# Order of VectorE's low parts and output additions in an encoder block's attention steps, and the queue of one input load

## The chip, the cores and the metric

The kernel runs on one core of one Trainium2 chip. The metric is the device time of one launch in microseconds (us); before the change three runs gave a median of 1334.39 us (1333.94 to 1335.63). PE is the matrix engine, PEld its weight load, DVE the vector engine, ACT the scalar (activation) engine, POOL GpSimd, SP the engine that issues most DMAs.

## The reference

An encoder block on 1024 tokens of width 1024, in float32: a layer norm, one wide input projection, two attention branches side by side (2-D neighbourhood attention with a bias table, 8 heads; sliding-window attention with a sink logit, 8 query heads on 2 key heads), gates, an output projection, and a squared-ReLU MLP, with two more layer norms.

```python
h = layer_norm(x, ln0_g, ln0_b)
proj = h @ w_in[l] + b_in[l]
qa, ka, va, qb, kb, vb, ga, gb = jnp.split(proj, IN_SPLITS, axis=-1)
...
y_na = neighbourhood_attention(qa, ka, va, na_rpb[l]) @ w_branch_na[l]
y_swa = windowed_gqa_with_sink(qb, kb, vb, swa_sink[l]) @ w_branch_swa[l]
mixed = jax.nn.sigmoid(ga) * y_na + jax.nn.sigmoid(gb) * y_swa
attn_out = mixed @ w_out[l] + b_out[l]
h = layer_norm(DEEPNORM_ALPHA * h + attn_out, ln1_g[l], ln1_b[l])
u = jnp.square(jax.nn.relu(h @ w_ff1[l] + b_ff1[l]))
h = layer_norm(DEEPNORM_ALPHA * h + u @ w_ff2[l] + b_ff2[l], ln2_g[l], ln2_b[l])
```

## The kernel before

Float32 accuracy is had from a faster matmul format by splitting every operand into a high part (rounded) and a low part (the rest), and adding two or three products. The high part is mostly made by ACT, the low part by DVE as "value minus high part".

**Start.** The input is loaded in eight tiles of 128 rows (`ln`, L172 to L177), the first of them in two halves, all by SP's queue; ACT's queue loads the identity (`ident`, L181). DVE takes the statistics of each tile (L129 to L131), POOL and ACT normalise it, PE transposes it, and ACT and DVE write it as high and low parts `hT` (L251 to L255). From there the projections run: `gemm3_steps` (L283) yields one matmul at a time, 24 to a half.

**Attention steps.** There are 16 heads (0 to 7 sliding window, 8 to 15 neighbourhood), of four steps each, each step two blocks of 128 queries. Between the matmuls of the steps the projections of later heads are filled in, 12 matmuls a step for the first eight heads and 18 for the others (`pump`). The order on every engine is the order of the code (the schedule is manual), and each engine works its queue off in that order. In step s, `steps` does, in this order:

- `part_a2(s + 1)`: DVE adds the sink's term, takes the reciprocal (L592, L593) and scales the exponentials (L596);
- `part_a(s + 2)`: PE makes the scores in two `ps_s` banks (L559, L560), DVE adds the bias and takes the maxima (L562, read out as a second instruction), and scales them (L568, L566 for neighbourhood heads);
- a quarter of the fill; then the deferred work that is marked early;
- `part_b(s)`: PE transposes the scaled exponentials into two `ps_t` banks (L618), ACT copies them as high parts `pth` (L621), ACT takes the exponentials of step s + 2 (L580, L583), DVE makes the low parts `ptl` (L624); then the deferred work that isn't PE's;
- 45% of the fill; `part_c(s - 1)`: PE multiplies with the values into a `ps_o` bank (L654); two steps make a pair that shares one bank, and there are two banks. At the end of a pair ACT copies one half of the bank to `oT` (L660) and DVE adds the other half (L663);
- all deferred work that is due; the rest of the fill.

**Deferred work.** `defer(n, f, ...)` puts f in a list; every fill matmul counts n down by one, and the next flush after it has reached 0 runs f. A flush "early" (ahead of part_b) takes only entries marked early. The neighbourhood projections use it for what follows a finished half: `evac` (three ACT copies out of the `ps_mm` bank) at once, and four matmuls later `evac2`, the low parts of q and k (L358, L360, L362), both early. Other deferred work on DVE: the low weights (`wlo`, L515), the rotary shuffles and low parts (L418, L471) and the values' low parts (`vv`, L332). The output addition L663 is deferred by 0, which is the flush right behind part_c.

**After the steps** DVE forms sums of operands for the gates' projections (a scheme with seven products in place of eight; L926 and around), then come the branch and output projections and the MLP (L1351, L1784), where PE has one matmul behind the other.

Of the kernel before, what the change touches and what calls it, by code (L numbers as in the profile page):

```python
# [47 lines left out]
D_NA = 4  # L48
# [35 lines left out]
def encoder_block(ctx, tc, x, w_in, w_br, w_out, w_ff1, w_ff2, par, rows, rpbp,  # L84
                  ident_d, masks_d, rope_d, out):
    nc = tc.nc
    PE, ACT, DVE, POOL = nc.tensor, nc.scalar, nc.vector, nc.gpsimd

    def b32(ap):
        return ap.bitcast(F32)  # L90
# [12 lines left out]
    def psum(tag):  # L103
        return pp.tile([P, 512], F32, tag=tag, name=f"ps_{tag}", bufs=PSB[tag])
# [16 lines left out]
    xv = x.rearrange("(g t) d -> g t d", g=NCG)  # L121
# [34 lines left out]
    ln = r3p.tile([P, 8, D], F32, tag="r3", name="ln")  # L156
# [14 lines left out]
    def ln0_load(half):  # L171
        for g in range(half * 4, half * 4 + 4):  # L172
            if g == 0:
                for n in range(2):
                    nc.sync.dma_start(ln[:, g, n * 512:(n + 1) * 512], xv[g][:, n * 512:(n + 1) * 512])
            else:
                nc.sync.dma_start(ln[:, g, :], xv[g])  # L177

    ln0_load(0)
    ident = cp.tile([P, P], F32, name="ident")  # L180
    nc.scalar.dma_start(ident, ident_d)  # L181
# [76 lines left out]
    def h_perm(part, k, half):  # L258
        return hT[:, part, k, half * 512:(half + 1) * 512]
# [17 lines left out]
    def gemm3_steps(ps, w, act):  # L277

        hi, lo = w[:2]
        for k in range(NK):  # L280
            for i, (a, b) in enumerate(((hi, 0), (hi, 1), (lo, 0))):
                yield
                PE.matmul(ps, a[:, k, :], act(b, k), start=(k == 0 and i == 0), stop=(k == NK - 1 and i == 2))  # L283
# [6 lines left out]
    def defer(*fns, pe=False, early=False):  # L290

        later.append([fns[0], fns[1:], pe, early])
# [48 lines left out]
    def proj_na_qk(h, w, store):  # L341
        q = ap.tile([P, S], F32R, tag="q", name="q", bufs=3)
        kh = ap.tile([P, S], F32R, tag="kh", name="kh")
        kl = ap.tile([P, S], F32R, tag="kl", name="kl")
        store.append((q, kh, kl))
        bq, bk = prm[0:64, C_QK + h:C_QK + h + 1], prm[64:P, C_QK + h:C_QK + h + 1]
        for half in range(2):
            cs = slice(half * 512, (half + 1) * 512)
            ps = psum("mm")
            yield from gemm3_steps(ps, w, lambda part, k: h_perm(part, k, half))  # L350

            def evac(cs=cs, ps=ps):
                ACT.activation(q[0:64, cs], ps[0:64, :], AF.Identity, bias=bq, scale=1.0)
                ACT.activation(kh[64:P, cs], ps[64:P, :], AF.Identity, bias=bk, scale=1.0)
                ACT.activation(kh[0:64, cs], ps[64:P, :], AF.Identity, bias=bk, scale=1.0)

            def evac2(cs=cs, ps=ps):
                DVE.scalar_tensor_tensor(out=q[64:P, cs], in0=ps[0:64, :], scalar=bq, in1=b32(q[0:64, cs]),  # L358
                                         op0=ALU.add, op1=ALU.subtract)
                DVE.scalar_tensor_tensor(out=kl[64:P, cs], in0=ps[64:P, :], scalar=bk, in1=b32(kh[64:P, cs]),  # L360
                                         op0=ALU.add, op1=ALU.subtract)
                DVE.tensor_copy(kl[0:64, cs], b32(kl[64:P, cs]))  # L362
            defer(0, evac, D_NA, evac2, early=True)


    mk = ap.tile([P, 640], F32, tag="mk", name="mk", bufs=1)
# [20 lines left out]

    n_rope = [0]
    in_steps, rope_ops = [], []

    def rope_step(p):

        if rope_ops:
            j = cp.tile([P, 1], F32, tag="junk", name="junk", bufs=2)
            POOL.tensor_copy(j, p[:, 0:1])
            rope_ops.pop(0)()
            if len(rope_ops) % 5 == 1:
                rope_ops.pop(0)()
                if rope_ops:
                    defer(8, rope_ops.pop(0))  # L400
# [147 lines left out]
    def part_a(s):  # L548

        hd, t = heads[s // 4], s % 4  # L550
        (q, kh, kl), _, _, bias_of, sink_h, _, _ = hd.get()
        st = ap.tile([P, 8], F32, tag="st", name="st", bufs=4)
        pns = []
        for i in range(2):
            j = 2 * t + i
            c0, c1 = max(j - 1, 0), min(j + 2, 8)
            n = (c1 - c0) * P
            ps = psum("s")
            PE.matmul(ps[:, :n], q[:, j * P:(j + 1) * P], kh[:, c0 * P:c1 * P], start=True, stop=False)  # L559
            PE.matmul(ps[:, :n], q[:, j * P:(j + 1) * P], kl[:, c0 * P:c1 * P], start=False, stop=True)  # L560
            p = ap.tile([P, 384], F32, tag="ss", name="ss", bufs=6)
            DVE.tensor_tensor_reduce(out=p[:, :n], in0=ps[:, :n], in1=bias_of(j), scale=1.0, scalar=NEG,  # L562
                                     op0=ALU.add, op1=ALU.max, accum_out=st[:, i:i + 1])
            pns.append((p, n, c0))
        if sink_h is None:
            DVE.tensor_scalar(out=st[:, 2:4], in0=st[:, 0:2], scalar1=-0.125, scalar2=None, op0=ALU.mult)  # L566
        else:
            DVE.tensor_scalar(out=st[:, 2:4], in0=st[:, 0:2], scalar1=snk8[:, sink_h:sink_h + 1],  # L568
                              scalar2=-0.125, op0=ALU.max, op1=ALU.mult)
        hd.pairs[t] = pns, st  # L570
# [14 lines left out]
    def part_a2(s):  # L585
        if s >= 64:
            return
        hd, t = heads[s // 4], s % 4
        pns, st = hd.pairs[t]
        sink_h = hd.get()[4]  # L590
        if sink_h is not None:
            DVE.tensor_tensor(out=st[:, 4:6], in0=st[:, 4:6], in1=st[:, 6:8], op=ALU.add)  # L592
        DVE.reciprocal(out=st[:, 6:8], in_=st[:, 4:6])  # L593
        for i in range(2):
            p, n, c0 = pns[i]
            DVE.tensor_scalar(out=p[:, :n], in0=p[:, :n], scalar1=st[:, 6 + i:7 + i], scalar2=None, op0=ALU.mult)  # L596
        rope_step(p)
# [29 lines left out]
    def part_c(s):  # L627

        hd, t = heads[s // 4], s % 4
        order, pth, ptl = hd.pairs[t]  # L630
        _, vv, vi, _, _, o_chunk, o_row = hd.get()
        if t % 2 == 0:
            hd.po = psum("o")
        po = hd.po

        runs = []
        for u, (c, i) in enumerate(order):
            if runs and runs[-1][0] == c:
                runs[-1][2] += 1
            else:  # L640
                runs.append([c, u, 1, i])
        runs.sort(key=lambda r: -r[2])
        runs.append(runs.pop(1))
        cols_ = (t % 2) * 256
        nmm = 0
        for c, u, w, i in runs:
            cc = slice(cols_ + i * P, cols_ + (i + w) * P)
            vs = vv[:, c, vi, :, :].rearrange("p a f -> p (a f)")
            main = (po[:, cc], vs, pth[:, u:u + w, :].rearrange("p u f -> p (u f)"))
            corr = (po[0:64, cc], vs[:, 0:64], ptl[:, u:u + w, :].rearrange("p u f -> p (u f)"))  # L650
            nmm += 1
            lastrun = nmm == len(runs)
            for m in ((corr, main) if lastrun else (main, corr)):
                PE.matmul(*m, start=(nmm == 1 and m is main), stop=(lastrun and m is main))  # L654
        if t % 2 == 1:

            oo = oT[o_row:o_row + 64, o_chunk, (t // 2) * 512:(t // 2 + 1) * 512]

            def evac():
                ACT.copy(oo, po[64:P, :])  # L660

            def evac2():
                DVE.tensor_tensor(out=oo, in0=po[0:64, :], in1=oo, op=ALU.add)  # L663
            if s == 63:
                last_evac.extend((evac, evac2))
            else:
                evac()
                defer(0, evac2)

    def fills():  # L670
        def na_v_of(hp):
# [28 lines left out]
    with tc.manual_schedule(engines=MANUAL):  # L700
# [83 lines left out]
        def steps(s, n, before_b=None, before_c=None):  # L784

            part = [int(n * SPLIT[0]), int(n * SPLIT[1])]
            part.append(n - sum(part))
            if 0 <= s + 1 < 64:
                part_a2(s + 1)
            if s + 2 < 64:  # L790
                part_a(s + 2)
            pump(part[0])
            if before_b:
                before_b()
            flush(False, True)
            if 0 <= s < 64:
                part_b(s, lambda: part_e(s + 2))
            elif s < 0:
                part_e(s + 2)
            flush(False)  # L800
            pump(part[1])
            if before_c:
                before_c()
            if s >= 1:
                part_c(s - 1)
            flush()
            pump(part[2])
# [371 lines left out]
        for f in range(8):  # L1179
            for half in range(2):  # L1180
# [8 lines left out]
                g, h = (f, 1) if half == 0 else (f + 1, 0)  # L1189
# [871 lines left out]
```

## Time and profile before

| | |
|---|---|
| median of three runs | 1334.39 us |
| the profiled execution, by itself | 1334.06 us |
| its span in the profile | 1332.3 us |
| granted PE clock | 0.998 |
| input, norm, first projections | 0 to 86 us |
| attention steps, 12 fill matmuls each | about 86 to 249 us |
| attention steps, 18 fill matmuls each | about 249 to 450 us |
| rest | 450 to 1332 us |

The page's first part gives each engine's busy time, its share of the span and its instructions. A row of the timeline has the start in us, the duration in us, the engine, the line, the operation, what is written from what, and, where the engine was idle before, how long and for whom in brackets. A row of the waits has the waiting engine and line, whom it waited for, the sum in us, the number and the longest. A row of the groups has the count, the busy time and the mean of one in ns, and the idle time before.

### The profile page before, as it was taken

The page shows a single profiled execution, that of the slowest core. Times are in us where ns is not written, and L with a number is a line of the kernel's source. Part 1 is how long each engine was busy: PE and PEld are TensorE (multiplying, and loading weights), DVE is VectorE, ACT ScalarE, POOL GpSimd, SP SyncE. Part 2 cuts the span into 40 slices and gives each one's busy share as a digit, 9 for nine tenths or more (in the row PEclk, how much of TensorE's full clock was granted, in tenths as well). Part 3 has the DMA queues.
Part 4 walks back from the last instruction along what each step waited for, and adds up shares of the span by engine and source line. Part 5 has one row for each costly group of instructions (what it writes and reads, how often), then busy time and mean ns, then how long its engine had stood idle before and what let it go on. Part 6 is the DMA issues. An engine that isn't in the chain of part 4 may idle for free.

```text
span 1332.3 us, 17348 instructions
## 1 busy us (share of the span) xinstructions
PE 1309.4 (98%) x6296; PEld 1088.7 (82%) x6296; DVE 985.0 (74%) x1618; ACT 710.1 (53%) x1231; POOL 282.4 (21%) x279
## 2 busy tenths in 40 slices
PE   8999998999999999999999999999999999999997
PEld 6788787888888878888888888888888888888886
DVE  7758888877877896444678987677655768787778
ACT  6446666766665535542445755555555543333346
POOL 4441221121120000344540012222100001111207
PEclk9999999999999999999999999999999999999999
DMA  6521111102101323656143576655528644544323
GB/s 226 187 87 49 48 52 41 38 23 47 51 23 40 127 94 118 223 190 221 70 152 134 169 242 205 210 196 187 205 100 311 221 190 150 213 150 174 127 103 127
DMA packets 66422, 183.94 MB, mean 138 GB/s; under 512 B 10400, under 2 KB 12064, under 8 KB 60576
## 3 DMA queue, kind: packets, MB, share of 16 engines
q1 hardware_dynamic: 65904, 182.38, 39.7%
q8 instruction: 49, 0.80, 0.3%
q10 hardware_dynamic: 432, 0.46, 0.1%
q14 instruction: 37, 0.30, 0.1%
HBM read 126.69 MB, written 56.31 MB: 137 GB/s over the span
## 4 chain that ended last, share of the span: by engine, by line
PE 80%; DVE 12%; ACT 3%; issue 1%; POOL 1%; DMA 1%; SPq 0%; DVEq 0%; ACTq 0%; POOLq 0%
PE ps_mm L283 13%; PE ps_mm L1351 7%; PE ps_t L1351 6%; PE ps_o L1351 6%; PE ps_mm L1784 6%; PE ps_s L1784 6%; PE ps_o L1784 5%; PE ps_t L1784 5%; PE ps_s L1351 3%; PE ps_t L618 2%; DVE ss L562 2%; PE ps_o L654 2%; ACT ss L580 2%; PE ps_mm L886 1%; DVE ss L596 1%
## 5 line engine op out<-in xcount | busy, mean ns | idle before, releaser
L283 PE MATMUL ps_mm<-hT,whi 128*128 128x512 f32 x832 | 269.5, 398 | 2.6 <-POOL hT L255 2.1
L283 PEld LDWEIGHTS ps_mm<-hT,whi 128*128 128x128 f32 x832 | 153.6, 188 | 30.2 <-POOL hT L255 3.5
L283 PE MATMUL ps_mm<-hT,wlo 128*128 128x512 f32 x416 | 166.9, 401 | 1.0 <-DVE wlo L717 1.0
L580 ACT ACTIVATE ss<-ss,st 128x384 f32<-128x384 f32 (+1 forms) x128 | 74.5, 583 | 62.1 <-DVE st L568 47.3
L1650 ACT CAST t<-stg 128x2048 fp32r<-128x2048 f32 x28 | 53.5, 1912 | 81.9 <-PE ps_o L1784 46.3
L1803 POOL TENSOR_TENSOR acc<-acc,rst 128x512 f32<-128x512 f32 x16 | 31.0, 1934 | 293.2 <-DMA rst<-xr_d 280.7
L1784 PE MATMUL ps_mm<-t,t 128*128 128x512 f32 x384 | 89.6, 389 | 0.0
L1784 PE MATMUL ps_s<-t,t 128*128 128x512 f32 x384 | 89.6, 389 | 0.0
L283 PEld LDWEIGHTS ps_mm<-hT,wlo 128*128 128x128 f32 x416 | 78.3, 188 | 12.4 <-DVE wlo L717 1.5
L1784 PEld LDWEIGHTS ps_mm<-t,t 128*128 128x128 f32 x384 | 72.1, 188 | 14.9
L1784 PEld LDWEIGHTS ps_s<-t,t 128*128 128x128 f32 x384 | 72.1, 188 | 14.9
L1351 PE MATMUL ps_t<-hS,tw 128*128 128x512 f32 x348 | 83.6, 389 | 0.0
L1351 PEld LDWEIGHTS ps_t<-hS,tw 128*128 128x128 f32 x348 | 65.3, 188 | 13.5
L621 ACT CAST pth<-ps_t 128x384 fp32r<-128x384 f32 (+1 forms) x128 | 51.8, 454 | 43.9 <-PE ps_t L618 43.2
L1653 DVE TENSOR_TENSOR t<-stg,t 128x2048 fp32r<-128x2048 f32 x28 | 65.6, 2341 | 12.9 <-ACT t L1650 12.9
L624 DVE TENSOR_TENSOR ptl<-ps_t,pth 128x384 fp32r<-128x384 f32 (+1 forms) x128 | 61.2, 517 | 17.1 <-ACT pth L621 16.5
L1173 POOL TENSOR_TENSOR mx<-sg 128x512 f32<-128x512 f32 x16 | 33.4, 2089 | 187.8 <-DVE sg L1172 187.8
L1784 PE MATMUL ps_t<-t,t 128*128 128x512 f32 x288 | 67.8, 390 | 0.6 <-DVE t L1653 0.6
L1784 PE MATMUL ps_o<-t,t 128*128 128x512 f32 x288 | 67.2, 389 | 0.0
L1784 PEld LDWEIGHTS ps_t<-t,t 128*128 128x128 f32 x288 | 53.9, 188 | 12.6 <-DVE t L1653 1.5
L1784 PEld LDWEIGHTS ps_o<-t,t 128*128 128x128 f32 x288 | 54.1, 188 | 11.2
L1627 POOL TENSOR_TENSOR rst<-rst,rr 128x512 f32<-128x512 f32 x16 | 22.4, 1400 | 187.3 <-DMA rst<-xn_d 116.0
(307 smaller groups left out, 3159.1 us busy)
## 6 DMA issues: line engine op xcount, KB each, us to landing
us_d<-usl SPq DMA_DIRECT2D x112, 256.0 KB
stg<-us_d SPq DMA_DIRECT2D x28, 1024.0 KB
raw<-in_w_ff SPq DMA_DIRECT2D x36, 512.0 KB
raw<-in_w_in SPq DMA_DIRECT2D x28, 512.0 KB
sg<-sg_d SPq DMA_DIRECT2D x32, 256.0 KB
w2b<-in_w_ff SPq DMA_DIRECT2D x7, 1024.0 KB
w2a<-in_w_ff SPq DMA_DIRECT2D x5, 1024.0 KB
sg_d<-sa SPq DMA_DIRECT2D x16, 256.0 KB
```

The lines of the kernel that those rows point to most:

```text
L283: PE.matmul(ps, a[:, k, :], act(b, k), start=(k == 0 and i == 0), stop=(k == NK - 1 and i == 2))
L562: DVE.tensor_tensor_reduce(out=p[:, :n], in0=ps[:, :n], in1=bias_of(j), scale=1.0, scalar=NEG, op0=ALU.add, op1=ALU.max, accum_out=st[:, i ...
L580: ACT.activation(p[:, :n], p[:, :n], AF.Exp, bias=st[:, 2 + i:3 + i], scale=0.125, accum_out=st[:, 4 + i:5 + i])
L618: PE.transpose(pt[:, (u - a) * P:(u - a + 1) * P], p[:, (c - c0) * P:(c - c0 + 1) * P], ident)
L621: ACT.copy(pth[:, a:b, :], pv)
L624: DVE.tensor_tensor(out=ptl[:, a:b, :], in0=pv, in1=b32(pth[:, a:b, :]), op=ALU.subtract)
L1173: POOL.tensor_tensor(out=mx[:, f, half * 512:(half + 1) * 512], in0=both[0], in1=both[1], op=ALU.add)
L1351: PE.matmul(ps, ww, act[:, part, k, :], start=(first and k == 0 and m == 0), stop=(k == 3 and m == 2), skip_group_check=True)
L1650: ACT.copy(slot[:, :, 0, :], src)
L1653: DVE.tensor_tensor(out=slot[:, :, 1, :], in0=src, in1=b32(slot[:, :, 0, :]), op=ALU.subtract)
L1784: PE.matmul(ps, st[:, a, part, j * P:(j + 1) * P], w[:, a, wpart, :], start=(first and a == 0 and m == 0), stop=(a == 3 and m == 2), skip_ ...
L1803: POOL.tensor_tensor(out=z, in0=z, in1=t, op=ALU.add)
```

## The change

Three edits. The first tile's second half is issued by ACT's queue, ahead of the identity. The neighbourhood low parts `evac2` are marked early only when the projection's half ends in step 32 or later. The output addition is deferred by 14 fill matmuls in place of 0.

```diff
     def ln0_load(half):
         for g in range(half * 4, half * 4 + 4):
             if g == 0:
-                for n in range(2):
-                    nc.sync.dma_start(ln[:, g, n * 512:(n + 1) * 512], xv[g][:, n * 512:(n + 1) * 512])
+                for n, q in enumerate((nc.sync, nc.scalar)):
+                    q.dma_start(ln[:, g, n * 512:(n + 1) * 512], xv[g][:, n * 512:(n + 1) * 512])
...
-            defer(0, evac, D_NA, evac2, early=True)
+            defer(0, lambda: (evac(), defer(D_NA, evac2, early=step_now[0] >= 32)), early=True)
...
     in_steps, rope_ops = [], []
+    step_now = [0]
...
                 evac()
-                defer(0, evac2)
+                defer(14, evac2)
...
             part.append(n - sum(part))
+            step_now[0] = s
             if 0 <= s + 1 < 64:
```

The order of instructions on PE and POOL stays the same; ACT has one DMA issue more and SP one less; on DVE no instruction comes or goes. The first place is DVE's queue at the end of a sliding-window step, the fifth pair's output addition before, with buffer numbers. Lines behind the change are one or two higher.

```order
L624 TENSOR_TENSOR ptl_1526<-ps_t_1527,pth_1525 128x384
L624 TENSOR_TENSOR ptl_1526<-ps_t_1531,pth_1525 128x384
L663 TENSOR_TENSOR oT_844<-ps_o_1492,oT_844 64x512
L592 TENSOR_TENSOR st_1510<-st_1510 128x2
L593 RECIPROCAL st_1510<-st_1510 128x2
```

The same place on DVE in the changed kernel:

```order
L625 TENSOR_TENSOR ptl_1525<-ps_t_1526,pth_1524 128x384
L625 TENSOR_TENSOR ptl_1525<-ps_t_1530,pth_1524 128x384
L664 TENSOR_TENSOR oT_844<-ps_o_1368,oT_844 64x512
L593 TENSOR_TENSOR st_1509<-st_1509 128x2
L594 RECIPROCAL st_1509<-st_1509 128x2
```

The slot is filled as before, but with the addition of the pair before (ps_o 1368, which is 1369 in the old numbering); the fifth pair's own comes two steps later, ahead of that step's low weights. With 18 fill matmuls it comes one step later, behind the next maxima and low parts.

The second place is DVE's queue where the first half of the first neighbourhood head's projection has ended, before:

```order
L568 TENSOR_SCALAR st<-st,snk_106 128x2
L358 SCALAR_TENSOR_TENSOR q<-ps_mm,prm,q 64x512
L360 SCALAR_TENSOR_TENSOR kl<-ps_mm,prm,kh 64x512
L362 CAST kl<-kl 64x512
L624 TENSOR_TENSOR ptl<-ps_t,pth 128x384 x2
L592 TENSOR_TENSOR st<-st 128x2
L593 RECIPROCAL st<-st 128x2
```

And in the changed kernel:

```order
L569 TENSOR_SCALAR st<-st,snk_106 128x2
L625 TENSOR_TENSOR ptl<-ps_t,pth 128x384 x2
L358 SCALAR_TENSOR_TENSOR q<-ps_mm,prm,q 64x512
L360 SCALAR_TENSOR_TENSOR kl<-ps_mm,prm,kh 64x512
L362 CAST kl<-kl 64x512
L593 TENSOR_TENSOR st<-st 128x2
L594 RECIPROCAL st<-st 128x2
```

The three operations of the neighbourhood head have gone behind the step's low parts. The same happens at two more halves, and from the fourth on the order is as before.

## Prediction

> **What bounds the kernel now.** I read the engine shares first, then busy time by stretch, then the start of each step's scores in the timeline, then who waits for whom in that stage.
>
> ```profile
> PE 1309.4 (98%) x6296; PEld 1088.7 (82%) x6296; DVE 985.0 (74%) x1618; ACT 710.1 (53%) x1231; POOL 282.4 (21%) x279
> 40.00:130.00 90.00, 89.91 (x451) 75.67 (x452) 63.99 (x141) 44.71 (x96) 29.22 (x24) 1.00 0.30 102
> 130.00:180.00 50.00, 48.69 (x286) 41.04 (x286) 42.90 (x126) 33.02 (x87) 11.26 (x17) 1.00 0.10 32
> 180.00:230.00 50.00, 47.31 (x274) 38.79 (x272) 42.22 (x119) 34.19 (x88) 10.55 (x16) 1.00 0.22 61
> 230.00:280.00 50.00, 48.12 (x280) 40.95 (x280) 39.33 (x114) 33.73 (x77) 7.46 (x15) 1.00 0.11 28
> 280.00:310.00 30.00, 30.00 (x169) 25.95 (x170) 26.51 (x65) 20.32 (x45) 6.30 (x9) 1.00 0.18 45
> ```
>
> Columns of a stretch: its length, then busy time of PE, PEld, DVE, ACT, POOL, then the clock and the DMA. The kernel is a TensorE kernel, but from 130 to 280 us PE is short of full by 1.3, 2.7 and 1.9 us (5.9 in all), while DVE is at 42.9 of 50, its highest share of any long stretch; from 280 us on PE is full. So only the attention steps of the first eight heads and a little of the ninth have anything to give. How much, the step length says better. These rows are the first scores matmul (L559) of every fourth step, that is of each head:
>
> ```profile
> 106.72 0.28 PE L559 MATMUL ps_s<-kh,q 128*128 128x256 f32 x1
> 125.63 0.29 PE L559 MATMUL ps_s<-kh,q 128*128 128x256 f32 x1
> 144.84 0.39 PE L559 MATMUL ps_s<-kh,q 128*128 128x256 f32 x1 [0.17 <-DVE st L562]
> 165.97 0.39 PE L559 MATMUL ps_s<-kh,q 128*128 128x256 f32 x1 [1.13 <-DVE st L562]
> 185.28 0.39 PE L559 MATMUL ps_s<-kh,q 128*128 128x256 f32 x1
> 206.82 0.38 PE L559 MATMUL ps_s<-kh,q 128*128 128x256 f32 x1 [1.55 <-DVE st L562]
> 228.52 0.28 PE L559 MATMUL ps_s<-kh,q 128*128 128x256 f32 x1
> 249.09 0.28 PE L559 MATMUL ps_s<-kh,q 128*128 128x256 f32 x1
> 299.97 0.28 PE L559 MATMUL ps_s<-kh,q 128*128 128x256 f32 x1
> 324.69 0.28 PE L559 MATMUL ps_s<-kh,q 128*128 128x256 f32 x1
> 374.36 0.28 PE L559 MATMUL ps_s<-kh,q 128*128 128x256 f32 x1
> 29.95 0.44 PE ps_o L242 x4
> ```
>
> A head with nothing in its way takes 125.63 - 106.72 = 18.91 us. The next ones take 19.21, 21.13, 19.31, 21.54, 21.70 and 20.57: over the floor by 0.30, 2.22, 0.40, 2.63, 2.79 and 1.66. The fifth of these holds two groups of four transposes for v, 0.44 each by the last row (a chain row of four transposes), so 1.91 remain. Later, two heads with 72 fill matmuls each take 374.36 - 324.69 = 49.67 with PE full; the pair 249.09 to 299.97 takes 50.88, so 1.21 over. **In all 0.30 + 2.22 + 0.40 + 2.63 + 1.91 + 1.66 + 1.21 = 10.3 us stand over the floor**, all before 300 us. That is the most that any reordering of DVE can return.
>
> The Trainium skill (Perfetto Trace Analysis, Identifying the Most-Contended Engine) calls matmul busy time a poor measure of headroom, since pipelined matmuls look otherwise in the trace, and asks for the weight loads' share. Here it decides a size: by matmul idle 5.9 us could come back, by the step lengths, which need no busy row, 10.3; the trace agrees with the page, PEld being at 41.0 of 50 in the same stretch.
>
> Who makes PE wait, and what DVE waits for (106 to 260 and 106 to 249 us):
>
> ```profile
> PEld ps_s L559 <- DVE st L562: 6.1, 9, 2.0
> PEld ps_t L618 <- DVE ptl L624: 5.3, 14, 1.5
> L663 DVE TENSOR_TENSOR oT<-ps_o,oT 64x512 f32<-64x512 f32 x14 | 9.6, 683 | 7.5 <-ACT oT L660 7.3
> ```
>
> Scores wait for the maxima (L562) that free a bank, transposes wait for the low parts (L624). DVE itself loses 7.3 us waiting in front of the output additions (L663) for ScalarE's copy of the same bank.
>
> **The change part by part.** *Output additions (L663).* One case in full:
>
> ```profile
> 171.73 0.28 ACT L583 ACTIVATE st<-st,prm 128x2 f32<-128x2 f32 x1
> 172.03 0.58 ACT L660 COPY oT<-ps_o 64x512 f32<-64x512 f32 x1
> 172.65 0.69 DVE L663 TENSOR_TENSOR oT<-ps_o,oT 64x512 f32<-64x512 f32 x1 [1.14 <-ACT oT L660]
> 177.58 0.16 DVE L592 TENSOR_TENSOR st<-st 128x2 f32<-128x2 f32 x1 [0.77 <-ACT st L583]
> ```
>
> The copy stands in ScalarE's queue behind two exponentials, so DVE is idle for 1.14 us, and behind the addition stand the next scaling, the maxima and the low parts, for which PE waits. After the change the addition in that slot belongs to the pair before, whose copy was done about two steps (10 us) ago: the wait goes, the 0.6 us of work stay. The next operation needs L583, started 171.73; the second row of that kind (177.58) carries the same dependence, and it leaves DVE about 1.1 us early. In the slots beside a low weight part (L515) the addition only changes sides with it: no gain. No instruction is added or taken away; 32 additions stay 32.
>
> The 1.14 us case comes six times in the 7.3 us above (6 x 1.14, and two short ones): once per head between 106 and 207 us, and last here:
>
> ```profile
> 235.56 0.68 DVE L663 TENSOR_TENSOR oT<-ps_o,oT 64x512 f32<-64x512 f32 x1 [1.14 <-ACT oT L660]
> ```
>
> What DVE gains reaches PE only up to the excess there. Heads 125 to 166: two waits, 2.28, against an excess of 2.52: **2.3**. Heads 166 to 207: 2.28 against 3.03: **2.3**. Between them (166 to 185 us) PE was only 0.40 over the floor; there the lead isn't lost but kept for the next long DVE step: the scores there arrive early enough for DVE to run up to a step ahead. Head 207 to 228 has no such wait; there DVE idles before the values' low part,
>
> ```profile
> 214.31 0.69 DVE L332 TENSOR_TENSOR vv<-ps_t,vv 128x512 fp32r<-128x512 f32 x1 [2.31 <-ACT vv L331]
> ```
>
> and the two additions, which now come ahead of such a step instead of behind it, disappear in that idle time: 2 x 0.6 = 1.2 at most, of an excess of 1.91; I take **1.0**.
>
> *Neighbourhood low parts (L358 to L362) late before step 32.* The transposes' longest waits are where these three stand in front of the low parts:
>
> ```profile
> L358 DVE SCALAR_TENSOR_TENSOR q<-ps_mm,prm,q 64x512 fp32r<-64x512 f32 x3 | 2.2, 745 | 0.1
> L360 DVE SCALAR_TENSOR_TENSOR kl<-ps_mm,prm,kh 64x512 fp32r<-64x512 f32 x2 | 1.5, 756 | 0.0
> L362 DVE CAST kl<-kl 64x512 fp32r<-64x512 f32 x2 | 0.8, 422 | 0.1
> 231.02 0.31 PEld L618 LDWEIGHTS ps_t<-ident,ss 128*128 128x128 f32 x3 [1.47 <-DVE ptl L624]
> 241.09 0.64 PEld L618 LDWEIGHTS ps_t<-ident,ss 128*128 128x128 f32 x5 [0.45 <-DVE ptl L624]
> 251.57 0.31 PEld L618 LDWEIGHTS ps_t<-ident,ss 128*128 128x128 f32 x3 [1.24 <-DVE ptl L624]
> ```
>
> Three groups move behind the low parts (the window ends within the third). The three operations take 0.745 + 0.756 + 0.422 = 1.9 us, so the low parts end up to 1.9 us earlier, more than each of these waits. The maxima behind both come neither earlier nor later. q and k of the first two neighbourhood heads are first read by the scores of step 32, at 249.09, and of the head after it, at least one step behind. With the wait of 1.14 at 235.56, head 228 to 249 could give its whole 1.66; I take **1.3**. The pair behind it could give 1.21; I take **1.0**. From step 32 on this edit changes nothing, and PE is full there: the later moved additions are at nothing, hidden by PE (30.00 of 30.00); if PE were not full they would cost 0.6 us each at most.
>
> *First tile's second half by ScalarE's queue.*
>
> ```profile
> 0.72 0.41 ACTq L181 DMA_DIRECT2D ident<-in_ident  x1
> 0.73 0.86 SPq L175 DMA_DIRECT2D ln<-in_x  x2
> 1.63 1.38 SPq L177 DMA_DIRECT2D ln<-in_x  x3
> 6.78 1.29 DVE L129 BATCH_NORM_STATS2 st<-ln 128x6 f32<-128x512 f32 x2 [1.26 <-DMA ln<-in_x]
> 4.50:5.00 0.50, 0.50 (x2) 0.33 (x1) 0.50 (x1) 0.00 (x0) 0.00 (x0) 1.00 0.74 303
> ```
>
> The second tile is the first one that the chain waits for (6.78), and its load is now issued 0.43 us sooner; everything behind it on SP's queue too, and the identity 0.41 later, with 6 us to spare. DMA isn't full at 4.5 us (0.74), so some of it arrives. Bounds: +0.43 gained; on the other side the two halves of the first tile now land together, and the first statistics can start later by the length of one half, 0.68 us, which the idle 1.26 before 6.78 swallows: 0. I take **0.3**. The Trainium skill (DMA: Bandwidth & Descriptors, Issuing engines are not separate DMA queues) holds that a second issuing engine saves sequencer time alone; by it the gain is also at most the 0.43 of one issue, and 0 had the engines been full.
>
> **Sum:** 2.3 + 2.3 + 1.0 + 1.3 + 1.0 + 0.3 = 8.2 us. The profiled execution took 1334.06 (span 1332.3), so 1325.9; the median of the runs shown is 1334.39, 0.33 above it, so 1326.2. Behind 300 us nothing stops the gain: PE is full, and the DVE stretch behind the last step starts from a low part that waits for PE, so it moves along.
>
> **Rivals.** *Only the direct waits shrink.* DVE's lead is lost at each wait for ScalarE (0.77 at 177.58), and PE gains only where a wait follows at once. For it: the head around 172.65, the place of a removed wait, is only 0.40 over the floor. Against it: DVE is at 43 of 50, with little other idle time. Price: the three low-part waits of 1.47 + 0.45 + 1.24 = 3.2, 0.3 at the start, and perhaps 1 behind the removed waits: 4.5, so 1329.9. Chance 22%.
>
> *The waits only change their name.* DVE meets ScalarE's statistics or PE instead, and the low parts' earlier end is taken back by a later wait: 0 to 2 us, 1332.4 to 1334.4. For it: PE's matmul row is idle only 5.9 us. Chance 9%.
>
> *The output bank is held too long: slower.* The addition frees a ps_o bank, and there are two. It now runs behind the low part two steps later, just ahead of the first matmul of the pair that reuses the bank:
>
> ```profile
> 170.50 1.01 DVE L624 TENSOR_TENSOR ptl<-ps_t,pth 128x384 fp32r<-128x384 f32 x2
> 174.06 0.28 PE L654 MATMUL ps_o<-pth,vv 128*128 128x256 f32 x1
> ```
>
> Low part done 171.51, addition done 172.2, first matmul 174.06: 1.9 us to spare. If DVE runs later than that against PE, each of the 14 pairs pays up to one addition, 0.68: 9.5 us, less what the waits return; about 1338 to 1344. PE must wait for the same low part anyway, so it decides only when under 0.7 us are left. Chance 4%.
>
> **How the numbers follow.** My forecast of 8.2 us has 65%, its own range 6 to 10 (1324.4 to 1328.4); the rivals have 22, 9 and 4%. The lower end is the whole excess and the whole start, 10.3 + 0.4: 1323.7, taken as 1323.4. The upper end reaches into the first rival: 1330.6. A measurement of this kernel tells about 0.2%, 2.7 us. Faster by more than that: 65 + 22 + 1 of the second = 88%; within: 8%; slower: 4%.
>
> **What would show it.** In the profile after: no wait of 1.1 us before L663; heads between 125 and 249 us at 19 to 20 us each; no wait of transposes above 0.5 us near 230 and 250; DVE's share of those stretches nearer 45 of 50; scores of step 32 some 7 us earlier; the first real matmul 0 to 0.4 us earlier; and no wait of L654 for L663. It would be wrong if the heads kept 21 us with DVE waiting for ScalarE elsewhere, or if later stages lost what was gained.

## The result, and the profile after

The changed kernel takes 1325.84 us (median of five runs, 1325.64 to 1326.19), the kernel before on the same chip 1335.57 (five runs). The ratio is 0.9931, 95% interval 0.9917 to 0.9944, so 7 to 11 us were gained. One of the 19 runs of the kernel before that stand beside e1_load to e4_add7 below took 1448.22 us at a granted clock of 0.85 and is left out of every figure. The profiled execution took 1326.13 (span 1324.3) against 1334.06 (span 1332.3): 7.9 less, where the sum of the prediction had 8.2.

First the engine shares and the same stretches as before, in the changed kernel (length, then busy time of PE, PEld, DVE, ACT, POOL, the clock, the DMA):

```profile
PE 1304.9 (99%) x6296; PEld 1088.7 (82%) x6296; DVE 988.3 (75%) x1618; ACT 709.6 (54%) x1231; POOL 281.8 (21%) x279
130.00:180.00 50.00, 50.00 (x304) 43.88 (x303) 46.09 (x135) 36.74 (x93) 11.88 (x18) 1.00 0.10 32
180.00:230.00 50.00, 48.76 (x295) 42.07 (x294) 44.49 (x129) 34.19 (x88) 9.40 (x14) 1.00 0.21 61
230.00:280.00 50.00, 49.41 (x289) 42.73 (x287) 40.75 (x110) 33.29 (x79) 8.46 (x16) 1.00 0.14 41
```

From 130 to 180 us PE is full now, with 304 matmuls in place of 286, and DVE has gone from 42.90 to 46.09 of 50. Between 180 and 280 us PE still lacks 1.24 + 0.59 = 1.8 us. Second, the first scores matmul of a head (L560 now), in the timeline of PE:

```profile
105.87 0.28 PE L560 MATMUL ps_s<-kh,q 128*128 128x256 f32 x1
124.77 0.28 PE L560 MATMUL ps_s<-kh,q 128*128 128x256 f32 x1
162.44 0.28 PE L560 MATMUL ps_s<-kh,q 128*128 128x256 f32 x1
181.27 0.28 PE L560 MATMUL ps_s<-kh,q 128*128 128x256 f32 x1
200.83 0.38 PE L560 MATMUL ps_s<-kh,q 128*128 128x256 f32 x1 [0.56 <-DVE st L563]
221.95 0.28 PE L560 MATMUL ps_s<-kh,q 128*128 128x256 f32 x1
240.77 0.28 PE L560 MATMUL ps_s<-kh,q 128*128 128x256 f32 x1
266.32 0.28 PE L560 MATMUL ps_s<-kh,q 128*128 128x256 f32 x1
291.28 0.28 PE L560 MATMUL ps_s<-kh,q 128*128 128x256 f32 x1
```

Heads 125 to 162 take 37.67 for two, at the floor; the next take 18.83, 19.56, 21.12, 18.82, and the pair behind them 50.51. Third, who waits for whom from 106 to 252 us, which are the steps that the kernel before has from 106 to 260 us:

```profile
DVE st L593 <- ACT st L584: 5.5, 8, 0.8
DVE vv L332 <- ACT vv L331: 1.7, 1, 1.7
PEld ps_s L560 <- DVE st L563: 1.0, 1, 1.0
PEld ps_mm L283 <- DVE kl L360: 0.8, 1, 0.8
PEld ps_t L328 <- DVE ptl L625: 0.7, 1, 0.7
PEld ps_t L619 <- DVE vv L332: 0.4, 1, 0.4
PEld ps_t L619 <- DVE ptl L625: 0.2, 1, 0.2
```

The scores waited 6.1 us (nine times) for the maxima, and now once, 1.0. The transposes waited 5.3 for the low parts, and now 0.2. One wait is new: PE's fill matmuls (L283) for the neighbourhood low part (L360). Fourth, the moved addition, all of them first, then the slot that the prediction worked out in DVE's timeline, and the step behind it:

```profile
L664 DVE TENSOR_TENSOR oT<-ps_o,oT 64x512 f32<-64x512 f32 x14 | 9.5, 678 | 0.2
167.45 0.67 DVE L664 TENSOR_TENSOR oT<-ps_o,oT 64x512 f32<-64x512 f32 x1
168.06 0.16 DVE L593 TENSOR_TENSOR st<-st 128x2 f32<-128x2 f32 x1
170.64 0.87 DVE L625 TENSOR_TENSOR ptl<-ps_t,pth 128x384 fp32r<-128x384 f32 x2
172.29 0.16 DVE L593 TENSOR_TENSOR st<-st 128x2 f32<-128x2 f32 x1 [0.78 <-ACT st L584]
```

The idle time before the addition has gone from 7.5 to 0.2 us. In the slot (167.45) neither the addition nor the sink's term behind it (168.06) waits. In the step behind, which has no addition, DVE meets the exponentials' sums (L584) and waits 0.78; this kind of wait was there before too, and the view of the same steps (106 to 260 us) of the kernel before lets one compare:

```profile
DVE st L592 <- ACT st L583: 4.9, 7, 0.8
DVE vv L332 <- ACT vv L331: 3.2, 2, 2.3
```

So 7.3 us of waits for ScalarE's copy went, the waits for the statistics grew by 0.6, and those for the values' high part shrank by 1.5. The waits did not change their name.

### The profile page after: what moved, and what is told of

Read it like the earlier page. It is cut to its first block, busy times and chain, and to the rows that moved or that the text cites. A ratio compares the mean times of both kernels' runs of the same rounds, so it can differ in the third digit from the quotient of the medians.

```text
span 1324.3 us, 17358 instructions
## 1 busy us (share of the span) xinstructions
PE 1304.9 (99%) x6296; PEld 1088.7 (82%) x6296; DVE 988.3 (75%) x1618; ACT 709.6 (54%) x1231; POOL 281.8 (21%) x279
## 4 chain that ended last, share of the span: by engine, by line
PE 77%; DVE 14%; ACT 3%; DMA 2%; issue 2%; POOL 1%; SPq 0%; DVEq 0%; ACTq 0%; POOLq 0%
PE ps_mm L283 13%; PE ps_mm L1353 7%; PE ps_o L1353 6%; PE ps_mm L1786 6%; PE ps_t L1353 6%; PE ps_s L1786 6%; PE ps_o L1786 5%; PE ps_t L1786 4%; PE ps_s L1353 3%; PE ps_o L655 2%; DVE ss L563 2%; PE ps_t L619 1%; PE ps_mm L888 1%; DVE ss L597 1%; ACT ss L581 1%
## 5 line engine op out<-in xcount | busy, mean ns | idle before, releaser
L283 PE MATMUL ps_mm<-hT,whi 128*128 128x512 f32 x832 | 269.5, 398 | 3.2 <-POOL hT L255 2.1
L283 PEld LDWEIGHTS ps_mm<-hT,whi 128*128 128x128 f32 x832 | 153.5, 188 | 31.2 <-POOL hT L255 3.5
L283 PE MATMUL ps_mm<-hT,wlo 128*128 128x512 f32 x416 | 166.7, 401 | 1.0 <-DVE wlo L718 1.0
L283 PEld LDWEIGHTS ps_mm<-hT,wlo 128*128 128x128 f32 x416 | 78.2, 188 | 12.5 <-DVE wlo L718 1.5
```

## The experiments

Each gets one profile; its times are medians of the runs given. "Steps" is the time from the first scores matmul of step 0 to that of step 36 (275.03 - 91.27 = 183.76 before), read from each run's timeline of PE; it leaves the start out, and holds all heads that the change could help.

| run | first real matmul | step 0 | step 36 | steps | gained | median, us | ratio to before |
|---|---|---|---|---|---|---|---|
| before | 15.47 | 91.27 | 275.03 | 183.76 | | | |
| the change | 14.61 | 90.42 | 266.32 | 175.90 | 7.86 | 1325.84 (5) | 0.9931 [0.9917, 0.9944] |
| the change again | 14.59 | 90.40 | 266.57 | 176.17 | 7.59 | 1326.01 (5) | 0.9930 [0.9918, 0.9943] |
| e1_load | 14.65 | 90.45 | 274.57 | 184.12 | -0.36 | 1333.55 (10) | 0.9989 [0.9980, 0.9999] |
| e2_add | 16.02 | 91.81 | 267.90 | 176.09 | 7.67 | 1327.69 (4) | 0.9946 [0.9930, 0.9962] |
| e3_low | 15.92 | 91.73 | 274.49 | 182.76 | 1.00 | 1334.02 (10) | 0.9992 [0.9982, 1.0002] |
| e4_add7 | 14.60 | 90.40 | 267.28 | 176.88 | 6.88 | 1326.58 (4) | 0.9938 [0.9922, 0.9954] |
| e5_whole | 15.11 | 90.94 | 266.78 | 175.84 | 7.92 | 1326.05 (1) | one run |
| e6_prm | 14.86 | 90.72 | 266.32 | 175.60 | 8.16 | 1325.78 (1) | one run |
| e7_thr28 | 14.68 | 90.49 | 267.62 | 177.13 | 6.63 | 1327.00 (4) | 0.9938 [0.9922, 0.9955] |
| e8_hold | 14.65 | 90.48 | 286.88 | 196.40 | -12.64 | 1346.21 (1) | one run |
| e9_light24 | 14.64 | 90.49 | 265.79 | 175.30 | 8.46 | 1325.31 (5) | 0.9924 [0.9911, 0.9938] |

The change, the change again, e5_whole and e6_prm have the same steps, and gain 7.6 to 8.2: a single profile is good to some 0.3 us here.

### One edit alone

**e1_load**, the kernel before with the start's edit only:

```diff
-                for n in range(2):
-                    nc.sync.dma_start(ln[:, g, n * 512:(n + 1) * 512], xv[g][:, n * 512:(n + 1) * 512])
+                for n, q in enumerate((nc.sync, nc.scalar)):
+                    q.dma_start(ln[:, g, n * 512:(n + 1) * 512], xv[g][:, n * 512:(n + 1) * 512])
```

> Only the first edit: the first tile's second half on ScalarE's queue, all else as before. Theory A (all of the 0.86 us by which the scores run early at 91 us in the changed kernel comes from this edit, and it stays to the end): first scores of step 0 at 90.4 us, heads 125 to 249 us as long as before (about 21.1, 19.3, 21.5, 21.7, 20.6), span about 0.9 us shorter, 1331.4. Rival (an early start is taken back by the deferred waits in the steps): first scores at 90.4, but the scores of step 36 back at 275 us.

The first real matmul comes at 14.65, 0.82 earlier, and step 0 too. Of this lead 0.36 us is missing at step 36, which is within what a single profile may be off. In the medians the edit is worth 1335.19 - 1333.55 = 1.6 us (1335.19 is the median of 18 runs of the kernel before), with an interval from 0.1 to 2.7.

**e2_add**, the kernel before with the addition's edit only:

```diff
-                defer(0, evac2)
+                defer(14, evac2)
```

> Only the output additions deferred by 14, all else as before. My sum: heads 125 to 166 give back 2.3 to 2.7 us, heads 166 to 207 2.3 to 2.5, head 207 to 228 0.6 to 1.0; from 228 on most of the low-part waits stay (1.5, 0.5, 1.2). Scores of step 36 some 6 us earlier than before's 275.0, span about 1326. Rival (only the direct waits shrink): 2 us or less from these heads, scores of step 36 at 273.

7.67 of the change's gain in the steps is here already. Its heads take 18.80, 18.79, 18.79 (126 to 183 us), 19.62, 21.14, 19.44. The neighbourhood low parts stand ahead of the steps' low parts as before, and of the waits that the prediction gave to them (1.47 + 0.45 + 1.24 = 3.16) 0.68 + 0.40 = 1.08 us are left without that edit. The waits of PEld from 106 to 255 us, and the two that stand at the places of the first and the third:

```profile
PEld ps_t L618 <- DVE ptl L624: 1.4, 4, 0.7
PEld ps_s L559 <- DVE st L562: 1.1, 1, 1.1
225.01 0.31 PEld L618 LDWEIGHTS ps_t<-ident,ss 128*128 128x128 f32 x3 [0.68 <-DVE ptl L624]
244.41 0.31 PEld L618 LDWEIGHTS ps_t<-ident,ss 128*128 128x128 f32 x3 [0.40 <-DVE ptl L624]
```

**e3_low**, the kernel before with the low parts' edit only:

```diff
-            defer(0, evac, D_NA, evac2, early=True)
+            defer(0, lambda: (evac(), defer(D_NA, evac2, early=step_now[0] >= 32)), early=True)
```

> Only the three groups of neighbourhood low parts moved behind the step's low parts. My sum: nothing before 228 us; then the waits of transposes of 1.5, 0.5 and 1.2 us are gone, worth 1.5 to 2.3 us at step 36 (scores at 272.7 to 273.5), span about 1330.5. Rival (they hold a ps_mm bank that the fill waits for, so the third group gives nothing): 1.0 to 1.5 us, with a wait of a fill matmul for L360 of about 0.8 us near 250 us.

1.00 us in the steps, so the lower end of the rival rather than the 1.5 to 2.3 of the sum, and a ratio that can't be told from 1. The waits of PEld from 106 to 275 us in this run, and the last of the new ones in its timeline:

```profile
PEld ps_s L560 <- DVE st L563: 6.4, 10, 2.0
PEld ps_t L619 <- DVE ptl L625: 2.2, 11, 0.3
PEld ps_mm L283 <- DVE kl L360: 1.7, 3, 0.8
251.85 0.30 PEld L283 LDWEIGHTS ps_mm<-hT,whi 128*128 128x128 f32 x2 [0.78 <-DVE kl L360]
```

The transposes no longer wait long, as planned, but the fill's matmuls do, three times, because q's and k's low parts are what frees the projection's `ps_mm` bank. The wait moved from one bank to another. In the changed kernel one of the three is left; DVE's and PE's rows at that place:

```profile
241.06 1.02 DVE L625 TENSOR_TENSOR ptl<-ps_t,pth 128x384 fp32r<-128x384 f32 x2
242.11 0.74 DVE L358 SCALAR_TENSOR_TENSOR q<-ps_mm,prm,q 64x512 fp32r<-64x512 f32 x1
242.87 0.76 DVE L360 SCALAR_TENSOR_TENSOR kl<-ps_mm,prm,kh 64x512 fp32r<-64x512 f32 x1
243.68 0.73 PE L283 MATMUL ps_mm<-hT,whi 128*128 128x512 f32 x2 [0.58 <-DVE kl L360]
```

L360 ends at 243.63 and the matmul starts at 243.68. Ahead of the two operations stands the step's low part, which is what the edit put there.

Singly the edits gain 1.6 + 7.5 + 1.2 = 10.3 us in the medians, together 9.1 to 9.7. In the steps the additions alone give 7.67, all together 7.59 to 8.16: the low parts' edit adds 0.5 at most, and nothing that these profiles can tell for certain. In heads it gains 0.62 (228 to 249 us: 18.82 against 19.44) and loses 0.42 behind it (25.55 against 25.13).

### Where the addition stands

**e4_add7**, the changed kernel with the addition deferred by 7 fill matmuls, so beside light steps rather than beside the low weights:

```diff
-                defer(14, evac2)
+                defer(7, evac2)
```

> The changed kernel with the additions deferred by 7 in place of 14: in the sliding-window steps they run one step after their pair, in the light steps without low weights, and not two. Theory A (what counts is that the copy is done and that the addition isn't ahead of the low weights): no wait for the copy either, the light steps hide the addition in DVE's 0.8 us wait for ScalarE, so heads 185 to 228 lose less of their 0.7 and 1.3 us over the floor: span 1323 to 1324.3. Rival (the slot matters, since the addition delays the next scaling in the light step): heads of 19.5 us and more, span 1325 to 1327.

Up to step 28 it is better by 0.89 (scores at 221.06 against 221.95), since the wait of the scores at 200.83 is gone. Then it loses 1.85: the light steps are those where the neighbourhood low parts stand. The last of the three waits for them:

```profile
244.64 0.30 PEld L283 LDWEIGHTS ps_mm<-hT,whi 128*128 128x128 f32 x2 [1.66 <-DVE kl L360]
```

0.82 of it was there with 14. Most of the rest is the addition, which in this run stands between the step's low part and L358 (242.38, 0.67 us).

**e8_hold**, the addition deferred by 26, so that it stands behind the low parts of the very step in which the pair that needs its bank again begins:

```diff
-                defer(14, evac2)
+                defer(26, evac2)
```

> The changed kernel with the additions deferred by 26: three steps after their pair, behind the low parts of the step in which the pair that reuses the bank begins. This is the rival by which the bank is held too long. If that rival has its price right: PE waits for L664 ahead of L655 once per pair in the sliding-window heads, up to 0.7 us and more each, 14 pairs, span 1330 to 1340. If the low part that PE waits for anyway covers it: no wait of L655 for L664, span 1324 to 1326.

This is the slower rival of the prediction, driven one step further: in the change the addition stands behind the low part of the step before that one, two steps after its pair. The waits of 106 to 262 us, and one of them in the timeline, with the addition that it waits for:

```profile
PE ps_o L655 <- DVE oT L664: 9.2, 6, 1.9
PE ps_o L655 <- ACT st L584: 7.0, 6, 2.1
124.70 0.68 DVE L664 TENSOR_TENSOR oT<-ps_o,oT 64x512 f32<-64x512 f32 x1
125.52 0.36 PE L655 MATMUL ps_o<-pth,vv 128*128 128x256 f32 x1 [1.95 <-DVE oT L664]
```

The addition ends at 125.38 and the pair's first matmul starts at 125.52, 1.95 late. From step 4 to step 32 this run takes 262.19 - 105.94 = 156.25 us and the change 240.77 - 105.87 = 134.90: 21.4 us for 14 pairs, 1.5 for each and not the 0.68 of one addition. That matmul uses the low parts of the step before (`part_c(s - 1)`), and now waits for the addition and so for the low parts of its own step too. Some of the waits are put down to ScalarE's L584 instead, but the addition is the only operation that this run moves.

### When the low parts go early again

**e7_thr28**, the changed kernel with the neighbourhood low parts early from step 28 on, so only the third group moved back:

```diff
-defer(D_NA, evac2, early=step_now[0] >= 32)
+defer(D_NA, evac2, early=step_now[0] >= 28)
```

> The changed kernel with the low parts early from step 28 on: the third group (whose half ends in step 28) is ahead of the step's low parts again. Theory A (the third group behind costs a wait of the fill for the ps_mm bank, 0.8 us at 243.7; ahead it costs the transposes' wait of 1.2 us less DVE's lead of 1 us): no wait for L360, transposes wait 0 to 0.5 us, scores of step 36 0.2 to 0.8 us earlier, span 1323.5 to 1324.1. Rival (DVE has no lead there): transposes wait 1.2 us again, scores of step 36 0.3 to 0.6 later.

Step 36 comes 1.05 to 1.3 us later than in the two profiles of the change. The `ps_mm` wait near 244 is gone and a longer one of the transposes is there:

```profile
244.16 0.31 PEld L619 LDWEIGHTS ps_t<-ident,ss 128*128 128x128 f32 x3 [1.87 <-DVE ptl L625]
```

So the third group costs PE either way, 0.82 or 1.87 in this order, and the edit's threshold of 32 is the better of the two.

### The start

**e5_whole**, the changed kernel with the first tile in one piece on SP's queue:

```diff
-                for n, q in enumerate((nc.sync, nc.scalar)):
-                    q.dma_start(ln[:, g, n * 512:(n + 1) * 512], xv[g][:, n * 512:(n + 1) * 512])
+                nc.sync.dma_start(ln[:, g, :], xv[g])
```

> The changed kernel with the first tile loaded whole, by one DMA on SP's queue; the second tile is issued as early as in the changed kernel (about 1.2 us), but on one queue. Theory Q (two queues, or halves on separate queues, move more bytes at once): the first real matmul is back near 15.4 us, with DVE waiting for the second tile again. Theory I (one issue less ahead of the second tile is what counts): the second tile's statistics follow the first's without a wait, first real matmul at about 14.6 to 15.0 us, the first tile's statistics at 4.3 us or later since both halves land together.

**e6_prm**, the halves on two queues as in the change, but with the load of `prm` issued ahead of the second tile, so that this is issued at 1.63 us, when the kernel before issues it:

```diff
+    prm = cp.tile([P, N_PAR], F32, name="prm")
...
+                nc.sync.dma_start(prm, par)
...
-    prm = cp.tile([P, N_PAR], F32, name="prm")
-    nc.sync.dma_start(prm, par)
```

> The changed kernel with the parameter load (77 KB) issued on SP's queue ahead of the second tile, so that the second tile is issued at about 1.6 us as before the change, while the first tile's halves still go by two queues. Theory Q: the gain at the start stays, less the 0.2 us that 77 KB take: first real matmul at 14.6 to 14.9 us. Theory I: the second tile lands at 6.5 us or later, DVE waits for it 0.5 us or more, first real matmul at 15.1 to 15.5 us.

The two runs speak for different theories: e5_whole has no wait for the second tile, as theory I said, and e6_prm has none either although that tile is issued late, as theory Q said. In e6_prm DVE's statistics of the second tile start at 6.16, in the change at 5.92 and in e5_whole at 6.42, in all three without a wait, where the kernel before waited 1.26 and started at 6.78. The first real matmul of e6_prm is at 14.86, so 0.61 of the change's 0.86 us stay without the second tile's earlier issue, which is worth 0.25 at most (the first tile's second half is still issued earlier there, as in the change). In e5_whole it is at 15.11: its first tile's statistics start at 4.78, when the whole tile has landed, and those of the change at 4.29. The last two columns of a stretch, the DMA's share and its GB/s, tell more. From 5 to 6 us, before:

```profile
5.00:6.00 1.00, 1.00 (x4) 0.79 (x3) 0.45 (x3) 0.85 (x1) 0.33 (x1) 1.00 0.78 250
```

In the change:

```profile
5.00:6.00 1.00, 1.00 (x6) 0.82 (x5) 0.93 (x4) 0.36 (x1) 0.00 (x0) 1.00 1.02 404
```

In e6_prm:

```profile
5.00:6.00 1.00, 1.00 (x4) 0.80 (x3) 0.93 (x4) 0.29 (x1) 0.00 (x0) 1.00 1.06 426
```

And in e2_add, which loads both halves on SP's queue like the kernel before:

```profile
5.00:6.00 1.00, 1.00 (x4) 0.79 (x3) 0.50 (x3) 0.80 (x1) 0.28 (x1) 1.00 0.73 234
```

e5_whole has 414 there, e3_low (both halves on SP) 131, and all eight profiles with the halves on two queues have 397 to 426. With two half tiles one behind the other on one queue the DMA falls to 131 to 250 GB/s for a microsecond, while the second tile is under way; with the halves on two queues, or the tile in one piece, it doesn't. Why it falls is open.

### A mixture of both

**e9_light24**, the changed kernel with the addition beside the light steps up to step 24 only, where they hold no neighbourhood low parts:

```diff
-                defer(14, evac2)
+                defer(7 if step_now[0] < 24 else 14, evac2)
```

> The addition stands in the slots beside the light steps up to step 24 and, as in the change, beside the low weight parts from there on. Theory (a DVE operation belongs where DVE has the lead, and the light slots lose only where the low parts of the neighbourhood stand): the head of steps 20 to 24 takes 18.84 us as with 7 for all (19.56 in the change), the one behind it 20.9 to 21.1, then 18.8 and 25.55 as in the change; scores of step 36 some 0.7 to 0.9 us earlier than the change's 266.32, span 1323.4 to 1323.6. Rival (the lead gained before step 24 is used up by the values' head, whose chain runs through ScalarE's copy, or by the heads behind it): step 36 at 266.1 to 266.4, span 1324.0 to 1324.4.

**after_again**, the changed kernel once more, on the same chip as e9_light24:

> The change once more beside it, for one chip: step 36 at 266.2 to 266.4, median within 0.5 us of 1325.84, both theories alike.

e9_light24's heads take 18.83 (163 to 181), 18.84, 21.18, 18.79 and 25.60; step 36 is 0.53 and 0.78 earlier than in the two profiles of the change, where 0.7 to 0.9 was expected beside the first; the head with the values takes 21.18 and not 20.9 to 21.1. On one chip the five runs lie from 1325.19 to 1325.52 and those of the change from 1325.94 to 1326.66, so it is 0.7 us faster. The waits of PEld that are left, 106 to 275 us:

```profile
PEld ps_t L328 <- DVE ptl L625: 1.1, 2, 0.9
PEld ps_mm L283 <- DVE kl L360: 0.9, 1, 0.9
PEld ps_t L619 <- DVE vv L332: 0.6, 2, 0.4
PEld ps_t L619 <- DVE ptl L625: 0.4, 2, 0.2
```

No scores matmul waits for maxima any more.

## Why the prediction was right, and where it was not

**Time, sign and the main mechanism** held: 1326.2 forecast, 1325.84 and 1326.01 measured. The time is nearer than the gain: the forecast took 8.2 us from the 1334.39 of three runs, and the five runs have 1335.57, so the medians gained 9.7. By the terms of the sum, from the profiled executions:

| term | forecast | measured |
|---|---|---|
| heads 125 to 166 | 2.3 | 40.34 - 37.67 = 2.67 |
| heads 166 to 207 | 2.3 | 40.85 - 38.39 = 2.46 |
| head 207 to 228 | 1.0 | 21.70 - 21.12 = 0.58 |
| head 228 to 249 | 1.3 | 20.57 - 18.82 = 1.75 |
| pair 249 to 300 | 1.0 | 50.88 - 50.51 = 0.37 |
| start | 0.3 | 15.47 - 14.61 = 0.86 |
| sum | 8.2 | 8.7 |

That the sums lie so close is in part luck: the heads up to 207 us, head 228 to 249 and the start came out 1.5 us above their terms together, the head 207 to 228 and the pair 1.05 below.

**The signs** that were named came, but for the start and for the head 207 to 228, which kept 21.12 where 19 to 20 was named: no wait of 1.1 us before the addition, the other heads at 18.8 to 19.6, no wait of the transposes above 0.5 us near 230 and 250, DVE at 46.09 and 44.49 of 50, the scores of step 32 8.3 us earlier (249.09 to 240.77).

**The additions.** The main step, that a removed wait in front of L663 comes back on PE and that DVE keeps the lead where PE doesn't need it, held. The two rivals against it fall with e2_add: its heads stand at 18.8 from 126 to 183 us, also the one that was only 0.40 over the floor, and the addition's edit alone gives 7.67 in the steps where "only the direct waits shrink" had 4.5 for the whole change. The floor of 18.91 was 0.1 too high; heads now take 18.8. One reading beside it was wrong: 42.9 of 50 isn't DVE's highest share. The prediction's own row from 280 us has 26.51 of 30, and from 430 to 480 us the kernel before has DVE at 45.15 of 50, both with PE full; what marks the place is PE's waits for DVE, not DVE's share.

**The low parts** are where the working failed. The step "three groups move behind the low parts ... more than each of these waits" took the transposes' waits near 231, 241 and 251 us for the cost of that order. e2_add shows that two thirds of them were DVE's lateness: once the additions no longer wait, the same order costs 1.08 us and not 3.16. And the step did not look at which bank the moved operations free. L358 and L360 read the `ps_mm` bank, and e3_low shows PE waiting for it three times. Of the 1.3 + 1.0 forecast for the two terms in which this edit stood 1.75 + 0.37 = 2.12 came, but e2_add has 1.94 of that by the additions alone (20.57 - 19.44 = 1.13 for the head, and 50.88 - 50.07 = 0.81 for the pair, 242.77 to 292.84 there). That these two terms came out nearly right was luck, since the cause was mostly another edit.

**Head 207 to 228.** 1.0 was mis-sized, 0.58 measured. The wait for the values' high part shrank as foreseen (2.31 to 1.72 at its longest, one wait in place of two), but PE waits there for a chain through ScalarE as well, at the transposes of the values (0.7) and behind `vv` (0.4). Even in e4_add7, which comes into this head without a late score, it takes 20.96.

**The start** broke its bound: 0.86 in the profile, and 0.8 to 1.4 if the changed starts (step 0 at 90.40 to 90.49 in seven profiles) are held against the three with the old one (91.27, 91.73, 91.81). The step "its load is now issued 0.43 us sooner" counted an issue time, and e6_prm, which takes that away for the second tile, keeps 0.61. The Trainium skill (DMA: Bandwidth & Descriptors, Issuing engines are not separate DMA queues), which the prediction weighed, says that more issuing engines save issue time only. The measurement differs for these two half tiles, 0.86 against 0.43. It agrees in another way: with the tile as one DMA, e5_whole moves 414 GB/s from 5 to 6 us on one queue where the change moves 404 on two, though its first statistics start 0.49 us later.

**The size of what was there.** The forecast took 10.3 us from step lengths rather than the 5.9 by which PE's busy time fell short. 7.6 to 8.2 us came back in the steps, more than 5.9, so the row of busy matmuls did hide headroom: PE's busy time fell from 1309.4 to 1304.9 us for the same 6296 matmuls. The trace agrees here with the Trainium skill (Perfetto Trace Analysis, Identifying the Most-Contended Engine), which calls matmul busy time no good measure of how close TensorE is to its limit and names the weight loads' share, among others, in its place. By that share the prediction's own rows would have said it: PEld takes 25.95 of 30 us from 280 us on, so 43.25 of 50, and is 2.2 + 4.5 + 2.3 = 9.0 us short of it from 130 to 280 us, which at this rate are 10.4 us of time, an estimate.

**The slower rival** stayed away because the addition at 14 is done in time for the bank's next pair, as the prediction had it: the addition of 167.45 ends at 168.12, and the pair's first matmul comes 2.2 us later (1.9 was forecast).

```profile
170.37 0.28 PE L655 MATMUL ps_o<-pth,vv 128*128 128x256 f32 x1
```

No wait of L655 is in the changed kernel's list. The rival's price of 0.68 for a pair isn't tested. e8_hold shows that a bank held too long does make PE wait, but there the addition stands one step later than in the rival, behind a low part that the pair's first matmuls don't need, so its 1.5 us for a pair are addition and low part together. In the change the low part ahead of the addition is the one that these matmuls need, so "PE must wait for the same low part anyway" holds there; it is the expectation of e8_hold that carried this sentence over to an order in which it doesn't.

**Behind step 36** the prediction said that nothing stops the gain. From step 36 to the span's end the kernel before takes 1332.3 - 275.03 = 1057.3 us, the changed one 1058.0 and 1057.5, and e1 to e4, e7, e8 and e9 from 1057.3 to 1057.7. So the 8.7 us at step 36 became 8.0 at the end in the first profile and 8.46 became 8.2 in the second. Nothing in this stretch was edited. "PE is full" isn't quite so there: PE waits 1.06 us for DVE's operands of the gates at 492.09 before, and 1.05 at 483.39 in the change, so this wait moved along whole. PE's later short waits say where the tenths go: at the one of 772.55 (763.83 in the change) the lead is still 8.72, at the one of 1181.51 (1173.64) it is 7.87. The stretch between these two takes 408.96 in the profile of before, 409.81 and 409.26 in the two of the change, and 409.08 to 409.49 in e1 to e4, e7 and e9. Before is the shortest of these nine and the change's first profile the longest, in a part that no edit touches; whether a few tenths are really given back there stays open.

## What to carry to other kernels

An operation that waits in an in-order queue costs its wait to all that stands behind it: move it to where its input has long been there, and look first which buffer it frees, since holding that one too long can cost more than the wait did (1.5 us a pair in e8_hold, against 1.14 for a wait). A lead of an engine is worth counting over several steps, not wait by wait. Before adding up the gains of two edits, ask whether the second one's waits are only the lateness that the first one takes away.

## What was not expected of the hardware

Loading one 512 KB tile as two halves of 256 KB on one queue let the DMA fall to 250, 234 and 131 GB/s from 5 to 6 us (three profiles), while the same halves on two queues ran at 397 to 426 there (eight profiles) and the tile in one piece at 414 (one profile), and the tile behind it was late by 1.26 to 1.75 us in the first case and in time in the others.
